# The delta rule's 128x128 inverse, by 32x32 diagonal squares in four corners of the array

## The chip, the cores and the metric

The kernel runs on one core of one Trainium2 chip. Its engines work side by side: TensorE (PE in the profile; PEld is its loading of weights), VectorE (DVE), ScalarE (ACT), GpSimd (POOL), and SyncE (SP), which starts most of the transfers. The metric is the time of one launch in device microseconds, the median of three runs.

## The reference

It is a trunk of two layers on a sequence of 256 tokens with 2048 channels, in float32. Each layer scales and shifts its normalised input by a modulation that is computed from `c`, mixes along the sequence, adds a gated residual, and follows with an MLP. Layer 0 mixes with eight heads of the gated delta rule and eight heads of chunk band attention, behind one combined input projection and ahead of one output projection; layer 1 mixes with a Mamba-2 scan (SSD). What the change touches is the triangular inverse in the delta rule:

```python
def gated_deltanet(q, k, v, z, b_raw, a_raw, conv_w, a_log, dt_bias, norm_w):
    ...
    lower = jnp.where(strict, jnp.einsum('bhnid,bhnjd->bhnij', kb, kc) * decay, 0.0)
    eye = jnp.eye(CHUNK, dtype=f32)
    tmat = lax.linalg.triangular_solve(eye + lower, jnp.broadcast_to(eye, lower.shape),
                                       left_side=True, lower=True, unit_diagonal=True)
    u = jnp.einsum('bhnij,bhnje->bhnie', tmat, vc * bc[..., None])
    w = jnp.einsum('bhnij,bhnjd->bhnid', tmat, kb * jnp.exp(gcum)[..., None])
    ...
def reference(x, c, mod_w, ...):
    c_act = jax.nn.silu(c)
    for layer in range(DEPTH):
        mod = jnp.einsum('bd,de->be', c_act, mod_w[layer]) + mod_b[layer]
        sh1, sc1, g1, sh2, sc2, g2 = [m[:, None, :] for m in jnp.split(mod, 6, axis=-1)]
        h = rms_norm(x, norm_mix_w[layer]) * (1.0 + sc1) + sh1
        ...
        x = x + g1 * mix
        h = rms_norm(x, norm_mlp_w[layer]) * (1.0 + sc2) + sh2
        x = x + g2 * sq_relu_mlp(h, mlp_w1[layer], mlp_w2[layer])
```

The kernel takes chunks of 128 tokens instead of the reference's 64, so that each of the eight heads has two 128x128 lower triangles to invert.

## The kernel before

**Projections.** Weights come in chunks of 1 MB (`raw`, four buffers, loaded by SP). Each chunk is split into a rounded half `wh` (ACT, a CAST, L332) and the rest `wl` (DVE, a subtraction, L336); the tokens' side is split in the same way (`u`). PE then multiplies (`mmx`, L322): 16 products of 512 columns with `wh`, which take both halves of `u` at once, and 16 of 256 columns with `wl`, which need only the rounded half of `u`. The name of the sum is `pw` or `pg`.

**The modulation** is not done on PE. A job (`mod_job`) loads 1 MB at a time into the same four `raw` buffers (`mraw`) and reduces each by one DVE instruction, L456. There are 192 of them over the kernel; `pump()` lets them go at a rate (`self.rate`, so many a quarter chunk) that is set stage by stage.

**What runs beside the projections.** A projection's chunk is issued in four quarters, with a `tick()` after each. A tick steps short tasks (`fast`), lets the background tasks take `bg_n` steps in turn (`bg_step`), and calls `pump()`. Background tasks are generators; each `yield` ends a step, and a step that yields `False` did nothing, so that the next task in turn is stepped. In the stage of the change `bg_n` is 1.5. A scheduler behind this then moves instructions within each engine's list by the readiness that it works out; the list that comes out is fixed, and each engine works through its own in order, with semaphores between them.

**The delta rule** is two background tasks, `gdn_group` 0 and 1, of four heads each; group 1 starts when group 0 is done. A group makes two tiles of 128 tokens (`gdn_tile`), each of which builds the strict lower triangle `gLt` for four heads (128x512) and inverts it: X starts as the identity minus the first subdiagonal of pairs, and level s (2, 4, 8, 16, 32, 64) joins blocks of s into blocks of 2s. Before, every level works on the full 128x128 of each head: a product of `gLt` and `gX` (L325 in `mm`), which DVE masks to the level's blocks (`gY`, L1131, after POOL has cleared the tile, L1130), a product with the transposed `gXt`, which DVE subtracts from X (L1137), then a transpose on PE (L329 in `tr`) and a copy by ACT into `gXt` (L1142). The last level goes into `gXt` straight away (L1146). The group goes on with `gvn`, `gS`, `gR`, `gqS` and `go`, whose transposes are the group's result; `gdn_z` puts the gate on it, and gives one of the four input units of the out projection. The flag `prep[0]` lets attention group 0 start.

**The out projection** takes its input units in the order 0, 2, 3, 1: a chunk holds two units, the first two chunks use units 0 and 2, and the third uses 3 (attention group 1) and 1 (delta rule group 1). `unit_of` steps a unit's tasks until they are done if its chunk comes first.

Of the kernel before, what the change touches and what calls it, by code (L numbers as in the profile page):

```python
# [12 lines left out]
I32 = mybir.dt.int32  # L13
AF = mybir.ActivationFunctionType
ALU = mybir.AluOpType
# [3 lines left out]
P = 128  # L19
# [93 lines left out]
class Trunk:  # L113
# [8 lines left out]
    def __init__(self, tc, ctx, ins, out):  # L122
# [14 lines left out]
        self.credit = self.fcredit = 0.0  # L137
        self.pending = self.early = self.etask = None
# [87 lines left out]

    def tick(self, quiet=False):
        self.fcredit = min(self.fcredit + self.fast_n, 3.0) if self.fast else 0.0
# [4 lines left out]
        n = len(self.bg)  # L233
# [167 lines left out]
    def masks(self):  # L401
        nc = self.nc
        g = nc.gpsimd
# [14 lines left out]

        self.M = {}
        for s in (2, 4, 8, 16, 32, 64):  # L420
            nb = P // (2 * s)
            m = self.const([P, nb, s], f"lev{s}")
            g.memset(m, 1.0)
            g.affine_select(out=m, in_=m, compare_op=ALU.is_ge, fill=0.0, base=-s, pattern=[[-2 * s, nb], [0, s]], channel_multiplier=1)
            g.affine_select(out=m, in_=m, compare_op=ALU.is_ge, fill=0.0, base=2 * s - 1, pattern=[[2 * s, nb], [0, s]], channel_multiplier=-1)
            self.M[s] = m

        self.M1T = self.const([P, 64, 2], "lev1T")
        g.memset(self.M1T, 0.0)
        v = self.M1T[:, :, 1:2]  # L430
        g.memset(v, 1.0)
        g.affine_select(out=v, in_=v, compare_op=ALU.is_equal, fill=0.0, base=0, pattern=[[-2, 64], [0, 1]], channel_multiplier=1)
        self.M1T = self.M1T.rearrange("p b c -> p (b c)")
# [613 lines left out]
    def gdn_tile(self, hg, t, kf, qf, vf, G):  # L1047
# [54 lines left out]

        xt = self.s2(tag="gXt")
        nc.vector.tensor_tensor(xt, lt, self.row(self.M1T), op=ALU.mult)
        nc.vector.tensor_tensor(xt, self.row(self.ident), xt, op=ALU.subtract)
# [8 lines left out]
        ps = self.pm()  # L1114
        for h in range(4):
            self.tr(ps[:, h], xt[:, h])
        x = self.s2(tag="gX")
        nc.scalar.copy(x, ps)
        G["X" + str(t)] = x
        yield  # L1120


        for s in (2, 4, 8, 16, 32, 64):
            nb = P // (2 * s)
            part = lambda a, n: a.rearrange("p h (b n c) -> p h b n c", n=2, c=s)[:, :, :, n]
            ps = self.pm()
            for h in range(4):
                self.mm(ps[:, h], lt[:, h], x[:, h])
            y = self.s2(tag="gY")
            nc.gpsimd.memset(y, 0.0)  # L1130
            nc.vector.tensor_tensor(part(y, 0), part(ps, 0), self.M[s].unsqueeze(1).to_broadcast([P, 4, nb, s]), op=ALU.mult)  # L1131
            yield
            ps = self.pm()
            if s < 64:
                for h in range(4):
                    self.mm(ps[:, h], xt[:, h], y[:, h])
                nc.vector.tensor_tensor(part(x, 0), part(x, 0), part(ps, 0), op=ALU.subtract)  # L1137
                yield
                ps = self.pm()
                for h in range(4):  # L1140
                    self.tr(ps[:, h], x[:, h])
                nc.scalar.copy(xt, ps)  # L1142
            else:
                for h in range(4):
                    self.mm(ps[:, h], y[:, h], xt[:, h])
                nc.vector.tensor_tensor(part(xt, 1), part(xt, 1), part(ps, 1), op=ALU.subtract)  # L1146
                yield
        G["Xt", t] = xt

    def gdn_group(self, hg, kc, qc, vc, gates):  # L1150
# [7 lines left out]
        while not all(t.done for t in tiles):  # L1158
            for t in tiles:
                if not t.done:  # L1160
                    t.step()
            if all("X" + str(n) in G for n in range(2)):
                self.prep[hg].done = True
            yield

# [659 lines left out]
```

## Time and profile before

| | us |
|---|---|
| median of three runs | 2698.53 (2694.78 to 2700.00) |
| the profiled execution, its own time | 2697.5 |
| its span | 2695.8 |
| PE busy in the span | 2638.6 (98%) |
| DVE busy in the span | 2154.2 (80%) |
| ACT busy in the span | 1348.0 (50%) |
| POOL busy in the span | 24.4 (1%) |
| mean granted clock of PE | 0.998 |

The profiler recorded one execution. Busy time is the time in which an engine works on at least one instruction; on PE many instructions are in flight at once, so a row's "mean ns of one" is a latency, and what one costs is the distance from one start to the next. Rows of groups read: line, engine, operation, output<-inputs by name, shape, count | busy us, mean ns of one | idle us of the engine just before them, and what ended most of it. Rows of waits read: engine, waiting tile and line <- engine, tile and line waited for: us in all, times, longest. Rows of the timeline read: start, duration, engine, instructions, count. Rows of stretches give for each engine the busy us and the instructions (x) in that stretch, then the granted clock and the share of the DMA engines.

### The profile page before, as it was taken

What the parts mean: (1) busy time and instruction counts of PE and PEld (TensorE: products, weight loads), DVE (VectorE), ACT (ScalarE), POOL (GpSimd) and SP (SyncE); (2) the same over time, 40 slices, a digit from 0 to 9 for tenths busy, and PEclk for the clock granted to TensorE, in tenths of its full rate; (3) what the DMA queues carried; (4) which work ended last, traced back from release to release, by engine and by line L of the source; (5) the groups of instructions that cost most, each with busy time, mean ns of one, the idle gap of its engine ahead of it and who ended that gap; (6) DMA issues with size and microseconds to landing.
All of it is one profiled execution on the core that took longest, in us unless ns stands there. A gap on an engine that the chain in (4) does not pass through costs nothing.

```text
span 2695.8 us, 40020 instructions
## 1 busy us (share of the span) xinstructions
PE 2638.6 (98%) x15834; PEld 2325.0 (86%) x15834; DVE 2154.2 (80%) x3106; ACT 1348.0 (50%) x1990; POOL 24.4 (1%) x98
## 2 busy tenths in 40 slices
PE   5999999999999999999999999999999999999999
PEld 4887989888888888888888888888888888888888
DVE  7998998997888888889889876897787855555554
ACT  3445455456345354454556544665555354454452
POOL 1000000000000000000000000000000000000000
PEclk9999999999999999999999999999999999999999
DMA  9986487868898898988555665554558855555553
GB/s 343 354 326 235 172 305 273 325 235 290 310 349 326 332 330 332 332 332 309 177 181 204 241 243 198 208 182 178 201 190 294 327 190 188 188 188 188 190 194 133
DMA packets 100459, 680.08 MB, mean 252 GB/s; under 512 B 11184, under 2 KB 14512, under 8 KB 19376
## 3 DMA queue, kind: packets, MB, share of 16 engines
q1 hardware_dynamic: 95376, 669.07, 68.0%
q10 hardware_dynamic: 4896, 8.46, 1.0%
q8 instruction: 124, 2.03, 0.3%
q14 instruction: 63, 0.52, 0.1%
HBM read 675.33 MB, written 2.16 MB: 251 GB/s over the span
## 4 chain that ended last, share of the span: by engine, by line
PE 91%; DVE 5%; DMA 1%; ACT 1%; issue 1%; SPq 0%; ACTq 0%; DVEq 0%
PE pw L322 71%; PE pg L322 13%; PE pm L325 3%; PE pm L322 2%; DVE mraw L456 2%; PE pm L329 1%; DVE wl L336 1%; DMA mraw<-in_mod_dram 1%; DVE u L1605 0%; ACT wh L332 0%; DVE hf L883 0%; DMA raw<-in_w_ab_dram 0%; DVE u L886 0%; DMA x<-in_x_dram 0%; DMA sd_rowd<-sd_rows 0%
## 5 line engine op out<-in xcount | busy, mean ns | idle before, releaser
L332 ACT CAST wh<-raw 128x1024 fp32r<-128x1024 f32 x870 | 906.0, 1051 | 999.4 <-PE pw L322 686.3
L336 DVE TENSOR_TENSOR wl<-raw,wh 128x1024 fp32r<-128x1024 f32 x870 | 1050.8, 1220 | 435.9 <-ACT wh L332 433.1
L322 PE MATMUL pw<-u,wh 128*128 128x512 f32 x5584 | 1320.0, 391 | 2.5 <-DVE u L886 1.3
L322 PEld LDWEIGHTS pw<-u,wh 128*128 128x128 f32 x5584 | 1031.9, 188 | 208.3 <-DVE x L948 1.5
L322 PEld LDWEIGHTS pw<-u,wl 128*128 128x128 f32 x5584 | 703.2, 192 | 21.8 <-issue 1.6
L322 PE MATMUL pw<-u,wl 128*128 128x256 f32 x5584 | 713.2, 284 | 0.7 <-DVE wl L336 0.7
L456 DVE SCALAR_TENSOR_TENSOR mraw<-mraw,crow 128x2048 f32<-128x2048 f32 x192 | 438.0, 2283 | 10.2 <-DMA mraw<-in_mod_dram 10.0
L322 PE MATMUL pg<-wh,u 128*128 128x512 f32 x864 | 278.8, 396 | 0.0
L322 PEld LDWEIGHTS pg<-wh,u 128*128 128x128 f32 x864 | 162.1, 188 | 32.7 <-issue 0.5
L948 DVE SCALAR_TENSOR_TENSOR x<-pw,mod,x 128x256 f32<-128x256 f32 x352 | 161.4, 478 | 33.0 <-PE pw L322 30.6
L322 PE MATMUL pg<-wl,u 128*128 128x512 f32 x432 | 170.0, 394 | 0.3 <-DVE wl L336 0.2
L322 PE MATMUL pg<-u,wh 128*128 128x256 f32 x672 | 124.5, 285 | 0.0
L322 PEld LDWEIGHTS pg<-u,wh 128*128 128x128 f32 x672 | 105.6, 192 | 0.3
L322 PEld LDWEIGHTS pg<-wl,u 128*128 128x128 f32 x432 | 81.3, 188 | 17.8 <-DVE wl L336 1.6
L322 PE MATMUL pg<-u,wl 128*128 128x256 f32 x336 | 95.4, 284 | 0.0
L322 PE MATMUL pm<-u,wh 128*128 128x256 f32 (+1 forms) x340 | 64.0, 292 | 19.2 <-ACT wh L332 19.2
L322 PEld LDWEIGHTS pm<-u,wh 128*128 128x128 f32 x340 | 54.2, 199 | 20.3 <-ACT wh L332 20.0
L322 PEld LDWEIGHTS pg<-u,wl 128*128 128x128 f32 x336 | 64.4, 192 | 0.0
L1007 DVE SCALAR_TENSOR_TENSOR u<-pad,cst,u 128x256 f32<-128x256 f32 x144 | 60.6, 479 | 4.7 <-ACT u L1001 4.7
L1511 ACT COPY rs<-pw 128x512 f32<-128x512 f32 x64 | 37.0, 578 | 34.5 <-PE pw L322 34.5
L885 ACT ACTIVATE u<-hf,mod 128x256 fp32r<-128x256 f32 x64 | 29.3, 502 | 48.4 <-DVE hf L883 48.4
L1512 DVE TENSOR_TENSOR rs<-pw,rs 128x512 f32<-128x512 f32 x64 | 43.8, 684 | 10.0 <-ACT rs L1511 10.0
(298 smaller groups left out, 1521.0 us busy)
## 6 DMA issues: line engine op xcount, KB each, us to landing
raw<-in_w_dram SPq DMA_DIRECT2D x256, 1024.0 KB, 5.1
mraw<-in_mod_dram SPq DMA_DIRECT2D x192, 1024.0 KB, 5.9
raw<-in_w_ab_dram SPq DMA_DIRECT2D x56, 1024.0 KB, 5.3
raw<-in_w_ssd_dram SPq DMA_DIRECT2D x48, 1024.0 KB, 4.9
raw<-in_w_sz_dram SPq DMA_DIRECT2D x32, 1024.0 KB, 4.9
raw<-in_wo_ssd_dram SPq DMA_DIRECT2D x32, 1024.0 KB, 4.9
raw<-in_wo_ab_dram SPq DMA_DIRECT2D x16, 1024.0 KB, 5.0
sE<-sd_rowd ACTq DMA_DIRECT2D x32, 256.0 KB, 4.2
```

The source lines that it names most:

```text
L322: return self.nc.tensor.matmul(o, a, b, start=start, stop=stop, skip_group_check=True)
L325: self.nc.tensor.matmul(o, lhsT, rhs, start=True, stop=True, skip_group_check=True)
L329: return self.nc.tensor.transpose(o, a, self.anti if flip else self.ident[:k, :k])
L332: a = self.nc.scalar.copy(hi, src)
L336: b = self.nc.vector.tensor_tensor(lo, src, hi.bitcast(F32), op=ALU.subtract)
L456: x = nc.vector.scalar_tensor_tensor(raw, raw, 1.0, self.crow, op0=ALU.mult, op1=ALU.mult, accum_out=t[:, f : f + 1])
L885: nc.scalar.activation(hi, h[:, f], AF.Identity, bias=shift[:, col])
L948: self.last = nc.vector.scalar_tensor_tensor(x[:, 2 * b + f], ps[:, f, n], g[:, 2 * cb + f : 2 * cb + f + 1], x[:, 2 * b + f], op0=ALU.mul ...
L1007: nc.vector.scalar_tensor_tensor(h, pad[:, f, 1 + q : 257 + q], w[:, q, j : j + 1], h, op0=ALU.mult, op1=ALU.add)
L1511: nc.scalar.copy(lo, ps[:, :, 1])
L1512: nc.vector.tensor_tensor(lo, ps[:, :, 0], lo, op=ALU.add)
```

## The change

`gdn_tile` ends when `gLt` and `gPt` are there. A new `gdn_inverse` then inverts both tiles of a group together, eight triangles at a time, and sets `G["Xt", t]` for the rest of the group, which is as before. It uses that X is block diagonal until level 16: only the four 32x32 squares on the diagonal are kept, one below the other, as a tile of 128x(8x32). Levels 2 to 16 multiply 32x32 squares, row group b of the array with column group b; DVE masks, subtracts and transposes (its own 32x32 transposes, in place of PE's). Level 32 joins pairs of squares, with four 32x32 corners written in place, and level 64 joins the two 64x64 halves. The masks are made once, and cut to their diagonal squares by copies on POOL. After each of its 13 steps the task yields `False` until three ticks have passed (`lag`), three quarters of a chunk; a task that is finished by force runs through up to 200 such yields a step without a tick. The flag `prep` is set after both tiles are done, ahead of the inverse.

```diff
--- before.py
+++ after.py
@@ -135,6 +135,7 @@
         self.fast, self.bg, self.open = [], [], []
         self.fast_n, self.bg_n = 0.5, 0.5
         self.credit = self.fcredit = 0.0
+        self.ticks = 0
         self.pending = self.early = self.etask = None
         self.pin = self.still = 0
         self.after_ins = self.gate = None
@@ -224,7 +225,16 @@
             t = self.fast.pop(0)
             t.finish()
 
+    def lag(self, n):
+
+        until = self.ticks + n
+        for _ in range(200):
+            if self.ticks >= until:
+                return
+            yield False
+
     def tick(self, quiet=False):
+        self.ticks += 1
         self.fcredit = min(self.fcredit + self.fast_n, 3.0) if self.fast else 0.0
         while self.fcredit >= 1:
             self.fcredit -= 1
@@ -416,21 +426,32 @@
+        def diagonal(name, full):
+
+            m = self.const([P, 32], name)
+            for b in range(4):
+                B = slice(32 * b, 32 * b + 32)
+                g.tensor_copy(m[B], full[B, B])
+            return m
+
+        self.I32 = diagonal("I32", self.ident)
...
+        for s in (2, 4, 8, 16):
+            full = self.s2([P, P], tag="lev")
...
+            self.M[s] = diagonal(f"lev{s}", full)
...
+        self.M1T = diagonal("lev1T", full)
@@ -1099,10 +1120,7 @@
         lt = self.s2(tag="gLt")
         for h in range(4):
             nc.vector.scalar_tensor_tensor(lt[:, h], ps[:, h], be[:, h : h + 1], E[:, h], op0=ALU.mult, op1=ALU.mult)
-
-        xt = self.s2(tag="gXt")
-        nc.vector.tensor_tensor(xt, lt, self.row(self.M1T), op=ALU.mult)
-        nc.vector.tensor_tensor(xt, self.row(self.ident), xt, op=ALU.subtract)
+        G["lt", t] = lt
         yield
         ps = self.pm()
         for h in range(4):
@@ -1111,41 +1129,89 @@
         nc.vector.tensor_tensor(p1, ps, E, op=ALU.mult)
         G["Pt", t] = p1
         yield
-        ps = self.pm()
-        for h in range(4):
-            self.tr(ps[:, h], xt[:, h])
-        x = self.s2(tag="gX")
-        nc.scalar.copy(x, ps)
-        G["X" + str(t)] = x
-        yield
-
-
-        for s in (2, 4, 8, 16, 32, 64):
-            nb = P // (2 * s)
-            part = lambda a, n: a.rearrange("p h (b n c) -> p h b n c", n=2, c=s)[:, :, :, n]
-            ps = self.pm()
-            for h in range(4):
-                self.mm(ps[:, h], lt[:, h], x[:, h])
-            y = self.s2(tag="gY")
-            nc.gpsimd.memset(y, 0.0)
-            nc.vector.tensor_tensor(part(y, 0), part(ps, 0), self.M[s].unsqueeze(1).to_broadcast([P, 4, nb, s]), op=ALU.mult)
-            yield
-            ps = self.pm()
-            if s < 64:
-                for h in range(4):
-                    self.mm(ps[:, h], xt[:, h], y[:, h])
-                nc.vector.tensor_tensor(part(x, 0), part(x, 0), part(ps, 0), op=ALU.subtract)
-                yield
-                ps = self.pm()
-                for h in range(4):
-                    self.tr(ps[:, h], x[:, h])
-                nc.scalar.copy(xt, ps)
+
+    def gdn_inverse(self, G):
+
+
+
+        nc = self.nc
+        lt = [G["lt", t] for t in range(2)]
+        heads = [(4 * t + h, t, h) for t in range(2) for h in range(4)]
+        B = [slice(32 * b, 32 * b + 32) for b in range(4)]
+        sub = [slice(4 * t, 4 * t + 4) for t in range(2)]
+        tile = lambda tag: self.s2([P, 8, 32], tag=tag)
+        flat = lambda a: a.rearrange("p n c -> p (n c)")
+        psum = lambda: self.pm([P, 512])[:, :256].rearrange("p (n c) -> p n c", c=32)
+        rep = lambda m, n: m.unsqueeze(1).to_broadcast([m.shape[0], n, 32])
+        xt, x = tile("gXt"), tile("gX")
+        for t in range(2):
+            for b in B:
+                nc.vector.tensor_tensor(xt[b, sub[t]], lt[t][b, :, b], rep(self.M1T[b], 4), op=ALU.mult)
+        nc.vector.tensor_tensor(xt, rep(self.I32, 8), xt, op=ALU.subtract)
+        nc.vector.transpose(flat(x), flat(xt))
+        XT = [self.s2(tag="gXT") for _ in range(2)]
+        x64 = self.s2([P, 8, 64], tag="gX6")
+        for z in XT:
+            nc.gpsimd.memset(z, 0.0)
+        nc.gpsimd.memset(x64[B[0], :, 32:], 0.0)
+        yield from self.lag(3)
+
+        for s in (2, 4, 8, 16):
+            ps = psum()
+            for n, t, h in heads:
+                for b in B:
+                    self.mm(ps[b, n], lt[t][b, h, b], x[b, n])
+            y = tile("gY")
+            nc.vector.tensor_tensor(y, ps, rep(self.M[s], 8), op=ALU.mult)
+            yield from self.lag(3)
+            ps = psum()
+            for n, t, h in heads:
+                for b in B:
+                    self.mm(ps[b, n], xt[b, n], y[b, n])
+            nc.vector.tensor_tensor(x, x, ps, op=ALU.subtract)
+            if s < 16:
+                nc.vector.transpose(flat(xt), flat(x))
             else:
-                for h in range(4):
-                    self.mm(ps[:, h], y[:, h], xt[:, h])
-                nc.vector.tensor_tensor(part(xt, 1), part(xt, 1), part(ps, 1), op=ALU.subtract)
-                yield
-        G["Xt", t] = xt
+                for t in range(2):
+                    for b in B:
+                        nc.vector.transpose(XT[t][b, :, b], x[b, sub[t]])
+            yield from self.lag(3)
+
+        ps = psum()
+        for n, t, h in heads:
+            for p in (0, 2):
+                self.mm(ps[B[p + 1], n], lt[t][B[p], h, B[p + 1]], x[B[p], n])
+        y = tile("gY")
+        for p in (0, 2):
+            nc.scalar.copy(y[B[p + 1]], ps[B[p + 1]])
+        nc.gpsimd.tensor_copy(x64[B[0], :, :32], x[B[0]])
+        nc.gpsimd.tensor_copy(x64[B[1], :, 32:], x[B[1]])
+        yield from self.lag(3)
+        ps = psum()
+        for n, t, h in heads:
+            self.mm(ps[B[1], n], XT[t][B[1], h, B[1]], y[B[1], n])
+            for p in (0, 2):
+                self.mm(ps[B[p], n], y[B[p + 1], n], XT[t][B[p + 1], h, B[p + 1]])
+        nc.vector.tensor_scalar(x64[B[1], :, :32], ps[B[1]], -1.0, None, op0=ALU.mult)
+        for t in range(2):
+            for p in (0, 2):
+                nc.scalar.activation(XT[t][B[p], :, B[p + 1]], ps[B[p], sub[t]], AF.Copy, scale=-1.0)
+        yield from self.lag(3)
+
+        lower, upper = slice(0, 64), slice(64, P)
+        ps = self.pm([P, 8, 64])
+        for n, t, h in heads:
+            self.mm(ps[upper, n], lt[t][lower, h, upper], x64[lower, n])
+        y = self.s2([P, 8, 64], tag="gY")
+        nc.scalar.copy(y[upper], ps[upper])
+        yield from self.lag(3)
+        ps = self.pm([P, 8, 64])
+        for n, t, h in heads:
+            self.mm(ps[lower, n], y[upper, n], XT[t][upper, h, upper])
+        for t in range(2):
+            nc.vector.tensor_scalar(XT[t][lower, :, upper], ps[lower, sub[t]], -1.0, None, op0=ALU.mult)
+            G["Xt", t] = XT[t]
+        yield from self.lag(3)
 
     def gdn_group(self, hg, kc, qc, vc, gates):
 
@@ -1159,9 +1225,9 @@
             for t in tiles:
                 if not t.done:
                     t.step()
-            if all("X" + str(n) in G for n in range(2)):
-                self.prep[hg].done = True
             yield
+        self.prep[hg].done = True
+        yield from self.gdn_inverse(G)
 
         ps = self.pm()
         for h in range(4):
```

The scheduler's lists then read as follows at three places. On PE, one level of group 0; `gX`, `gLt`, `gY`, `gXt` are the inverse's tiles, `pg` is a projection. Before:

```order
L329 MATMUL pm_2762<-ident,gX_2546 128x128 x4
L325 MATMUL pm_2768<-gX_2546,gLt_2495 128x128 x4
L329 MATMUL pm_2776<-ident,gX_2553 128x128 x4
L325 MATMUL pm_2782<-gX_2553,gLt_2508 128x128 x4
L322 MATMUL pg_2702<-hw_1725,raw_2557 128x256
L329 MATMUL pm_2790<-anti,as_2738 128x128
L322 MATMUL pg_2838<-wh_2686,u_286 128x512
...
L325 MATMUL pm_2806<-gY_2773,gXt_2500 128x128 x4
L325 MATMUL pm_2812<-gY_2787,gXt_2513 128x128 x4
```

After:

```order
L335 MATMUL pm_2909<-gX_2577,gLt_2521 32x32 x16
L335 MATMUL pm_2909<-gX_2577,gLt_2531 32x32 x16
L332 MATMUL pg_2870<-wh_2854,u_787 128x512
L332 MATMUL pg_2870<-wl_2855,u_787 128x512
L332 MATMUL pg_2870<-wh_2854,u_787 128x512
L332 MATMUL pg_2870<-wh_2858,u_788 128x512
...
L332 MATMUL pg_2870<-wl_2859,u_788 128x512
L335 MATMUL pm_2987<-gY_2942,gXt_2576 32x32 x32
L332 MATMUL pg_2870<-wh_2858,u_788 128x512 x2
```

The transposes are gone from PE, each product became 32 small ones, and the projection's products lie between the two steps of a level, since a step is three quarters of a chunk behind the last.

On PE, ahead of the out projection's third chunk, which writes the sum `pw_4819` before and `pw_5000` after; its inputs are the units 3 and 1 (`u_4931`, `u_4932`, `u_4857`, `u_4858` before; `u_5219`, `u_5220`, `u_5145`, `u_5146` after). Before:

```order
L322 MATMUL pw_4885<-u_4544,wl_4812 128x256 x4
L322 MATMUL pw_4885<-u_4545,wl_4812 128x256 x4
L322 MATMUL pw_4885<-u_4828,wl_4816 128x256 x4
L322 MATMUL pw_4885<-u_4829,wl_4816 128x256 x4
L322 MATMUL pw_4819<-u_4931,wl_4878 128x256 x4
L322 MATMUL pw_4819<-u_4932,wl_4878 128x256 x4
L322 MATMUL pw_4819<-u_4857,wl_4882 128x256 x4
L322 MATMUL pw_4819<-u_4858,wl_4882 128x256 x4
```

After:

```order
L335 MATMUL pm_5080<-gR_5068,gXT_4010 128x128 x3
L335 MATMUL pm_5088<-gvn_5054,gPt_3975 128x128 x3
L332 MATMUL pw_5173<-u_4617,wl_4993 128x256 x4
L335 MATMUL pm_5099<-gvn_5085,gPt_3982 128x128 x4
L332 MATMUL pw_5173<-u_5009,wl_4997 128x256 x4
L332 MATMUL pw_5173<-u_5010,wl_4997 128x256 x4
L339 MATMUL pm_5133<-ident,go_5093 128x128 x4
L339 MATMUL pm_5139<-ident,go_5104 128x128 x4
L332 MATMUL pw_5000<-u_5219,wl_5166 128x256 x4
L332 MATMUL pw_5000<-u_5220,wl_5166 128x256 x4
```

Before, the second chunk runs straight into the third. After, the end of group 1's chain (`gR` by `gXT`, `gvn` by `gPt`, the transposes of `go`) lies inside the second chunk and immediately ahead of the third.

On DVE, in the same place; `mraw` is the modulation job. Before:

```order
L456 SCALAR_TENSOR_TENSOR mraw_4919,mod_126<-mraw_4919,crow 128x2048
L1238 SCALAR_TENSOR_TENSOR cvt_4843<-cvt_4843,pg_4479 128x512
L1248 SCALAR_TENSOR_TENSOR u_2707<-cvt_4842,cst,u_2707 128x512
L1248 SCALAR_TENSOR_TENSOR u_2707<-cvt_4843,cst,u_2707 128x512
L336 TENSOR_TENSOR wl_4878<-raw_4875,wh_4877 128x1024
L336 TENSOR_TENSOR u_4857<-u_2707,u_4857 128x2x256
L336 TENSOR_TENSOR u_4858<-u_2707,u_4858 128x2x256
L336 TENSOR_TENSOR wl_4882<-raw_4875,wh_4881 128x1024
L336 TENSOR_TENSOR wl_4924<-raw_4921,wh_4923 128x1024
L336 TENSOR_TENSOR wl_4928<-raw_4921,wh_4927 128x1024
L336 TENSOR_TENSOR u_4931<-u_3463,u_4931 128x2x256
L336 TENSOR_TENSOR u_4932<-u_3463,u_4932 128x2x256
```

After:

```order
L287 SCALAR_TENSOR_TENSOR goy_5116<-got_5118,goy_5116 128x8
L1284 TENSOR_TENSOR goy_5116<-goy_5116,gor_5110 128x8
L1286 TENSOR_TENSOR go_5093<-go_5093,goy_5116 128x512
L1286 TENSOR_TENSOR go_5104<-go_5104,goy_5116 128x512
L477 SCALAR_TENSOR_TENSOR mraw_5412,mod_126<-mraw_5412,crow 128x2048
L1314 SCALAR_TENSOR_TENSOR u_2730<-cvt_5023,cst,u_2730 128x512
L1314 SCALAR_TENSOR_TENSOR u_2730<-cvt_5024,cst,u_2730 128x512
L346 TENSOR_TENSOR u_5145<-u_2730,u_5145 128x2x256
L346 TENSOR_TENSOR u_5146<-u_2730,u_5146 128x2x256
L346 TENSOR_TENSOR u_5219<-u_3375,u_5219 128x2x256
L346 TENSOR_TENSOR u_5220<-u_3375,u_5220 128x2x256
```

Before, the delta rule's rows lie far above. After, its last rows (`goy`, `go`) and a modulation instruction stand just ahead of the splits of `u` that the third chunk needs; the splits `wl` of that chunk stand far above them. By these rows DVE has issued 69 modulation instructions before and 73 after.

More of the change, by code (lines that the diff above doesn't have):

```diff
@@ L417, in masks @@
         g.affine_select(out=self.anti, in_=self.anti, compare_op=ALU.is_equal, fill=0.0, base=1 - P, pattern=[[1, P]], channel_multiplier=1)
+        def diagonal(name, full):
[5 more added lines that the diff above has]
+        self.I32 = diagonal("I32", self.ident)
         self.M = {}
-        for s in (2, 4, 8, 16, 32, 64):
+        for s in (2, 4, 8, 16):
+            full = self.s2([P, P], tag="lev")
+            v = full.rearrange("p (b n c) -> p b n c", n=2, c=s)[:, :, 0]
             nb = P // (2 * s)
[L422 to L430, printed above, removed]
+            g.memset(full, 0.0)
+            g.memset(v, 1.0)
+            g.affine_select(out=v, in_=v, compare_op=ALU.is_ge, fill=0.0, base=-s, pattern=[[-2 * s, nb], [0, s]], channel_multiplier=1)
+            g.affine_select(out=v, in_=v, compare_op=ALU.is_ge, fill=0.0, base=2 * s - 1, pattern=[[2 * s, nb], [0, s]], channel_multiplier=-1)
+            self.M[s] = diagonal(f"lev{s}", full)
+        full = self.s2([P, P], tag="lev")
+        v = full.rearrange("p (b c) -> p b c", c=2)[:, :, 1:2]
+        g.memset(full, 0.0)
         g.memset(v, 1.0)
         g.affine_select(out=v, in_=v, compare_op=ALU.is_equal, fill=0.0, base=0, pattern=[[-2, 64], [0, 1]], channel_multiplier=1)
-        self.M1T = self.M1T.rearrange("p b c -> p (b c)")
+        self.M1T = diagonal("lev1T", full)
     def mod_start(self, layer):
@@ L1113, in gdn_tile @@
         yield
-        ps = self.pm()
-        for h in range(4):
-            self.tr(ps[:, h], xt[:, h])
-        x = self.s2(tag="gX")
-        nc.scalar.copy(x, ps)
-        G["X" + str(t)] = x
-        yield
-        for s in (2, 4, 8, 16, 32, 64):
-            nb = P // (2 * s)
-            part = lambda a, n: a.rearrange("p h (b n c) -> p h b n c", n=2, c=s)[:, :, :, n]
-            ps = self.pm()
-            for h in range(4):
-                self.mm(ps[:, h], lt[:, h], x[:, h])
-            y = self.s2(tag="gY")
-            nc.gpsimd.memset(y, 0.0)
-            nc.vector.tensor_tensor(part(y, 0), part(ps, 0), self.M[s].unsqueeze(1).to_broadcast([P, 4, nb, s]), op=ALU.mult)
-            yield
-            ps = self.pm()
-            if s < 64:
-                for h in range(4):
-                    self.mm(ps[:, h], xt[:, h], y[:, h])
-                nc.vector.tensor_tensor(part(x, 0), part(x, 0), part(ps, 0), op=ALU.subtract)
-                yield
-                ps = self.pm()
-                for h in range(4):
-                    self.tr(ps[:, h], x[:, h])
-                nc.scalar.copy(xt, ps)
-            else:
-                for h in range(4):
-                    self.mm(ps[:, h], y[:, h], xt[:, h])
-                nc.vector.tensor_tensor(part(xt, 1), part(xt, 1), part(ps, 1), op=ALU.subtract)
-                yield
```

## The prediction

> **What bounds the kernel now.** I read the page's shares first, then busy time by stretch, then what DVE waits for, and last the instructions on either side of one moment.
>
> ```profile
> PE 2638.6 (98%) x15834; PEld 2325.0 (86%) x15834; DVE 2154.2 (80%) x3106; ACT 1348.0 (50%) x1990; POOL 24.4 (1%) x98
> ```
>
> By this line PE is the bound: work taken from it would come off the time one for one. The share is a mean, though, so the stage that the change touches has to be looked at by itself. The two groups of the delta rule lie between about 262 and 497 us.
>
> ```profile
> core 0: us, PE busy (x) PEld busy (x) DVE busy (x) ACT busy (x) POOL busy (x), PEclk, DMA share, GB/s
> 262.00:497.00 235.00, 232.20 (x1612) 211.71 (x1611) 220.34 (x451) 121.13 (x282) 12.75 (x31) 1.00 0.70 253
> 497.00:570.00 73.00, 73.00 (x420) 64.55 (x419) 71.95 (x102) 34.78 (x46) 0.00 (x0) 1.00 0.92 340
> 570.00:600.00 30.00, 27.39 (x163) 24.28 (x161) 25.93 (x61) 16.79 (x30) 0.00 (x0) 0.94 0.47 171
> ```
>
> In the stage PE is busy 232.2 of 235 us, and DVE 220.3: two engines are nearly full, and DVE has 14.7 us of slack. This is what it waits for there:
>
> ```profile
> DVE wl L336 <- ACT wh L332: 5.3, 8, 1.5
> DVE gR L1183 <- PE pm L325: 2.0, 1, 2.0
> DVE as L1313 <- issue: 1.7, 1, 1.7
> DVE ass L1270 <- ACT pg L1267: 1.6, 1, 1.6
> DVE gvn L1170 <- PE pm L325: 1.0, 1, 1.0
> DVE mraw L456 <- DMA mraw<-in_mod_dram: 0.6, 1, 0.6
> DVE gY L1131 <- PE pm L325: 0.6, 3, 0.2
> DVE goss L1214 <- ACT pm L1208: 0.4, 1, 0.4
> ```
>
> The squares' own chain (gY) waits 0.6 us in all: other work lies in its gaps. The largest wait, 5.3 us for the rounded half of a weight chunk, is a wait for PE at one remove, since ACT may write wh only when PE has done with the buffer.
>
> The stage ends where the third chunk of the out projection starts:
>
> ```profile
> 489.62 3.82 PE L322 MATMUL pw<-u,wh 128*128 128x512 f32 x16
> 492.85 3.48 DVE L336 TENSOR_TENSOR wl<-raw,wh 128x1024 fp32r<-128x1024 f32 x3
> 493.27 4.12 PE L322 MATMUL pw<-u,wl 128*128 128x256 f32 x33
> 496.26 1.28 DVE L336 TENSOR_TENSOR u<-u,u 128x512 fp32r<-128x512 f32 x2
> 497.22 3.82 PE L322 MATMUL pw<-u,wh 128*128 128x512 f32 x16
> ```
>
> The last two rows are the point. The wide products at 497.22 need the first of the two DVE instructions at 496.26, which ends at about 496.9. So DVE hands over 0.3 us before PE asks: the engines reach the end of the stage together. A chunk costs PE 16 x 0.228 (489.62 to 493.27) + 16 x 0.120 (33 in 3.95) = 5.55 us, and from here to 570 PE is busy 73.00 of 73.00. Each engine's instructions after about 600 us stand in the same order in both kernels, so the change is worth the shift of this one point.
>
> **What PE sheds.**
>
> ```profile
> 275.02 1.86 PEld L325 LDWEIGHTS pm<-gX,gLt 128*128 128x128 f32 x16
> 276.81 0.53 PEld L325 LDWEIGHTS pm<-u,u 128*128 128x128 f32 x4
> ...
> L325 PE MATMUL pm<-gX,gLt 128*128 128x128 f32 x192 | 25.2, 275 | 0.0
> L325 PE MATMUL pm<-gY,gXt 128*128 128x128 f32 x160 | 20.0, 275 | 0.0
> L325 PE MATMUL pm<-gXt,gY 128*128 128x128 f32 x32 | 4.1, 275 | 0.0
> L329 PE MATMUL pm<-ident,gX 128*128 128x128 f32 x80 | 12.3, 273 | 0.0
> L329 PE MATMUL pm<-ident,gXt 128*128 128x128 f32 x16 | 2.4, 274 | 0.0
> ```
>
> The 275 ns of one are latency; sixteen start within 1.79 us (275.02 to 276.81), 0.112 each. 192 + 160 + 32 + 96 = 480 instructions go, 53.7 us of PE.
>
> In their place come 592 products of 32x32 and 32 of 64x64; a float32 product is two instructions here (192 for 96 products), so 1184 and 64. Before has none of these shapes. Nearest are the 64-column products of the second layer:
>
> ```profile
> 1397.79 1.29 PE L322 MATMUL pw<-u,wh 128*128 128x512 f32 x5
> 1399.01 1.15 PE L325 MATMUL pm<-sx,sE 128*64 128x64 f32 x32
> 1400.10 2.11 PE L322 MATMUL pw<-u,wh 128*128 128x512 f32 x8
> ```
>
> 32 start in 1.09 us, 0.034 each, with entering and leaving the narrow shape inside it. I take half for half the columns, 0.016: 1184 x 0.016 = 18.9; the 64x64 ones at 0.034 give 2.2. Entering and leaving: five wide ones ahead of that group should take 5 x 0.228 = 1.14 and take 1.22, and eight behind take 1.94 (to the next start at 1402.04) instead of 1.82, so at least 0.2 us is lost a visit. There are 24 visits and about four split ones; at 0.2 to 0.35 that is 6 to 10, taken as 9. Together 30 us, so PE sheds about 23. Ends: at 0.008 a square, 33; at 0.034, 2; at 0.068 (twice the row: the small shape gains nothing and no square runs beside another), a loss of 40.
>
> [...]
>
> **What DVE sheds and gets.**
>
> ```profile
> L1131 DVE TENSOR_TENSOR gY<-pm,lev 128x256 f32<-128x256 f32 x24 | 9.8, 417 | 0.6 <-PE pm L325 0.6
> L1137 DVE TENSOR_TENSOR gX<-gX,pm 128x256 f32<-128x256 f32 x20 | 8.1, 413 | 0.2
> L1146 DVE TENSOR_TENSOR gXt<-gXt,pm 128x256 f32<-128x256 f32 x4 | 1.6, 414 | 0.0
> L1104 DVE TENSOR_TENSOR gXt<-gLt,lev1T 128x512 f32<-128x512 f32 x4 | 2.7, 684 | 0.0
> L1105 DVE TENSOR_TENSOR gXt<-ident,gXt 128x512 f32<-128x512 f32 x4 | 2.7, 681 | 0.0
> L1101 DVE SCALAR_TENSOR_TENSOR gLt<-pm,gbe,gE 128x128 f32<-128x128 f32 x16 | 5.0, 342 | 0.0
> L456 DVE SCALAR_TENSOR_TENSOR mraw<-mraw,crow 128x2048 f32<-128x2048 f32 x192 | 438.0, 2283 | 10.2 <-DMA mraw<-in_mod_dram 10.0
> ```
>
> The first five rows go: 9.8 + 8.1 + 1.6 + 2.7 + 2.7 = 24.9. Added are 64 instructions: 32 of 256 elements a lane at 0.414 = 13.2, and 32 of 128 at 0.342 (L1101, a dearer form) = 10.9; 24.1, or a little less. I take a net -2. Of the 64, 24 are transposes, an operation that no row shows; priced like the others they are 8 x 0.414 + 16 x 0.342 = 8.8. Ends: half (-4.4) and double (+8.8). [...]
>
> The order brings a larger term. The pacing pushes group 1's last levels and all that follows them into the first two chunks of the out projection, forced there since the third needs its result. More of the modulation job has been let through by then: ahead of the third chunk's splits DVE has 73 of the L456 instructions, against 69 before. That is 4 x 2.283 = +9.1 us of DVE work ahead of the point that ends the stage, and four more 1 MB loads ahead of it on SP's queue; the DMA share of 0.70 has room for 4 MB more in 235 us (17 GB/s on 253).
>
> **The other queues.**
>
> ```profile
> L1142 ACT COPY gXt<-pm 128x512 f32<-128x512 f32 x20 | 11.7, 583 | 15.9 <-PE pm L329 15.8
> L1118 ACT COPY gX<-pm 128x512 f32<-128x512 f32 x4 | 2.3, 582 | 5.7 <-PE pm L329 5.7
> mraw<-in_mod_dram SPq DMA_DIRECT2D x192, 1024.0 KB, 5.9
> ```
>
> ACT loses these copies (14.0 us) and gets seven a group back, six of them at most half as wide, under 6 us; at 121 of 235 us it paces nothing. POOL loses 24 memsets and gets ten small operations, and is busy 12.75 of 235 us. The masks' extra copies stand at the start of the kernel, far ahead of what uses them. The last row is the load that each of the four L456 instructions brings along. No instruction waits for `lag` itself: it only changes the order.
>
> **The sum.** DVE work to the point: 220.3 + 9.1 - 2.0 = 227.4 us. Slack: the 5.3 and the 1.7 go, as PE now is some 23 us lighter than DVE's pace needs; the rest that has a name is 2.0 + 1.6 + 1.0 + 0.6 + 0.6 + 0.4 = 6.2, and it stays, because the forced tail has the same steps (gvn, gR, goss), with large splits and modulation between most of them. I add 0.6 for the rounding on ACT that DVE's last four instructions now wait for, since the tail ends immediately ahead of them. 262 + 227.4 + 6.2 + 0.6 = 496.2, against 496.9: -0.7 us. PE's side is 262 + 232.2 - 23 + 2.8 = 474: PE would wait for DVE. The profiled execution took 2697.5 us, 1.0 below the median of the runs, so the forecast is 2697: PE's saving turns into PE waiting.
>
> **The rivals.**
> - PE's saving counts. For it speaks PE's 98%; against it, that DVE cannot finish its list before 262 + 227.4 = 489.4 with no slack at all, so at most 7.5 us can come, 2690; with transposes at their lower end 4.4 more, 2685. Only if DVE's instructions themselves ran faster, say for want of POOL's 12.75 us beside them, would the full 23 show: 2675.
> - A transpose costs half of what its neighbours do: -0.7 - 4.4 = -5.1, 2692. Nothing in the profile speaks for or against it. [...]
> - The tail is serial. Levels 16, 32 and 64 and eight more steps hand over between PE, ACT and DVE with nothing but two chunks beside them. If DVE's slack stays at 14.7 in spite of a faster PE, the point moves to 262 + 227.4 + 14.7 + 0.6 = 504.7, +7.8: 2705; with transposes at double, 2714. It turns slower once the slack passes 13 us. At 570 to 600, where the next layer part starts, PE idles 2.6 of 30 us and the granted clock is 0.94: a longer PE idle could cost clock as well.
> - The squares don't run beside each other, and the change doesn't do what it says. At 0.034 each PE ends at 262 + 232.2 - 2 + 2.8 = 495, beside DVE, and the forecast stands; at 0.068 it has 262 + 232.2 + 40 + 2.8 = 537: +40, 2737. It is slower than DVE from about 0.036 on. [...]
>
> **How the numbers follow.** About 0.2%, 5.4 us, is what a measurement here can tell: faster is below 2693.1, slower above 2703.9. DVE's pace with slack between 3 and 12: 0.58, itself 2693 to 2702. The transposes cheap or the slack nearly gone, 2685 to 2693: 0.20. The full PE gain: 0.05. The serial tail: 0.12. Squares at over 0.04 us: 0.05. The first spills over both bounds, by 0.08 to the fast side and 0.05 to the slow one. Faster 0.33, same 0.45, slower 0.22. The range is 2685 to 2707; the full PE gain, the far part of the serial tail and the slow squares stay outside.
>
> **What would show it.** If I am right: PE's busy share between 262 and 497 falls from 0.988 to about 0.9, with PE idle put down to DVE (wl and u); DVE's share rises to 0.96 or more; the third chunk's wide products start at 496 to 497; each level takes PE about 1.0 us for its 64 square instructions. Wrong: the stretch from 497 on begins 5 us earlier or later, a transpose far from 0.41 us, or 64 squares in 3 us.

## The result, and the profile after

The changed kernel takes 2717.8 us (median of six runs, 2716.0 to 2719.0), 1.0074 times the kernel before, 95% interval 1.0064 to 1.0084: about 20 us slower, where 2697 and at most 2707 were forecast. The profiled execution has a span of 2716.9 us.

The shares of the page say nothing of it. PE has shed 10 us over the whole kernel and DVE is as busy as before:

```profile
PE 2628.6 (97%) x16602; PEld 2301.7 (85%) x16602; DVE 2155.6 (79%) x3114; ACT 1342.3 (49%) x1980; POOL 30.2 (1%) x106
```

The stage ended before where the third chunk's wide products start, at 497.22 us; now they start at 517.14, 19.9 us later. Busy time by stretch, cut at 513, just before PE takes up the third chunk; the last row ends with DVE's last split of `u` for that chunk, at 514.9:

```profile
core 0: us, PE busy (x) PEld busy (x) DVE busy (x) ACT busy (x) POOL busy (x), PEclk, DMA share, GB/s
262.00:513.00 251.00, 218.04 (x2360) 185.23 (x2358) 227.19 (x465) 111.66 (x268) 7.12 (x15) 0.91 0.69 257
262.00:480.00 218.00, 196.63 (x2184) 166.48 (x2182) 199.60 (x411) 99.79 (x235) 7.12 (x15) 0.93 0.70 264
480.00:513.00 33.00, 21.42 (x177) 18.75 (x177) 27.59 (x55) 11.87 (x33) 0.00 (x0) 0.78 0.58 213
513.00:570.00 57.00, 56.44 (x313) 50.15 (x314) 49.17 (x68) 26.03 (x37) 0.00 (x0) 0.95 0.69 257
262.00:514.92 252.92, 219.40 (x2366) 186.59 (x2365) 229.11 (x468) 112.97 (x272) 7.12 (x15) 0.91 0.69 258
```

To its last split of `u` DVE is busy 229.1 us, and 227.4 were forecast; but it idles 252.9 - 229.1 = 23.8 us, and 6.8 were forecast. Of these, 18.4 us (218.0 - 199.6) lie ahead of 480 us and 5.4 between 480 and 513. PE idles too, 11.6 of 33 us in the last stretch, and its granted clock there is 0.78. In both kernels the work can be followed by DVE's splits wl, which come in the same number and order. Two stretches between the same splits, the 59th to the 105th (which opens the second chunk of the out projection), and the 105th to the 113th (four chunks on), before:

```profile
213.50:483.70 270.20, 266.42 (x1773) 234.67 (x1771) 248.21 (x545) 137.56 (x368) 13.48 (x34) 1.00 0.67 246
483.70:507.10 23.40, 23.40 (x137) 20.74 (x137) 22.47 (x28) 13.68 (x21) 0.00 (x0) 1.00 0.92 333
```

and after:

```profile
212.80:470.80 258.00, 235.93 (x2233) 195.21 (x2232) 231.69 (x506) 119.32 (x326) 6.95 (x18) 0.94 0.69 259
470.80:528.10 57.30, 45.16 (x446) 38.75 (x445) 44.66 (x86) 24.42 (x56) 1.72 (x2) 0.82 0.50 178
```

At the 105th split the changed kernel is 12.9 us ahead, with 16.5 us of DVE's work put off; eight splits later it is 21.0 behind. Counted on DVE's list, which adds up the loss but doesn't explain it, of these 21.0 DVE's work is 5.7 (276.4 against 270.7, most of it modulation moved ahead), its idle time 4.3 in the first stretch and 11.7 in the second, less 0.7 at the start. The largest waits of PE and of DVE between 480 and 517 us:

```profile
PE pm L339 <- DVE go L1286: 6.1, 1, 6.1
PE pw L332 <- ACT u L342: 4.2, 1, 4.2
DVE wl L346 <- ACT wh L342: 2.8, 1, 2.8
DVE mraw L477 <- DMA mraw<-in_mod_dram: 0.8, 1, 0.8
```

and the same place in the timeline, where the chain of PE, ACT and DVE can be read line by line:

```profile
500.07 1.19 PE L332 MATMUL pw<-u,wl 128*128 128x256 f32 x8
501.54 2.29 DVE L477 SCALAR_TENSOR_TENSOR mraw<-mraw,crow 128x2048 f32<-128x2048 f32 x1
502.90 0.19 ACT L1274 ACTIVATION_READ_ACCUMULATOR pm<-go 128x1 f32 x1
503.75 0.16 DVE L1280 TENSOR_TENSOR goss<-goss,gor 128x8 f32<-128x8 f32 x1
...
506.56 1.29 DVE L1286 TENSOR_TENSOR go<-go,goy 128x512 f32<-128x512 f32 x2
507.40 1.94 PE L339 MATMUL pm<-ident,go 128*128 128x128 f32 x8 [6.14 <-DVE go L1286]
508.71 2.29 DVE L477 SCALAR_TENSOR_TENSOR mraw<-mraw,crow 128x2048 f32<-128x2048 f32 x1 [0.85 <-DMA mraw<-in_mod_dram]
509.38 0.59 ACT L1294 COPY u<-pm 128x512 f32<-128x512 f32 x1 [0.27 <-PE pm L339]
510.92 1.41 DVE L1314 SCALAR_TENSOR_TENSOR u<-cvt,cst,u 128x512 f32<-128x512 f32 x2
511.70 2.33 ACT L342 CAST u<-u 128x512 fp32r<-128x512 f32 x4 [1.74 <-DVE u L1314]
513.56 3.78 PE L332 MATMUL pw<-u,wl 128*128 128x256 f32 x16 [4.22 <-ACT u L342]
517.14 4.68 PE L332 MATMUL pw<-u,wh 128*128 128x512 f32 x16
```

PE runs dry at 501.3, waits for the normalisation of go, transposes it, and waits again for the gated and rounded u. The first wait, 6.1 us, is a row of small steps: ACT's sums of squares, the last of which ends at 503.09, small DVE instructions of 0.2 us each from 503.75 to 506.56, and the first of the two that write `go`. DVE also has a modulation instruction of 2.3 us each time ahead of what PE waits for (501.54, 508.71), but most of each is hidden: by these rows the first holds the chain up by about 0.7 us (503.09 to 503.75), the second by about 0.95 (from the end of ACT's copy, 509.97, to 510.92).

### The profile page after: what moved, and what is told of

The parts are those of the page before. It is cut to its first block, busy times and chain, and to the rows that moved or that the text cites. A ratio compares the mean times of both kernels' runs of the same rounds, so it can differ in the third digit from the quotient of the medians.

```text
span 2716.9 us, 41519 instructions
## 1 busy us (share of the span) xinstructions
PE 2628.6 (97%) x16602; PEld 2301.7 (85%) x16602; DVE 2155.6 (79%) x3114; ACT 1342.3 (49%) x1980; POOL 30.2 (1%) x106
## 4 chain that ended last, share of the span: by engine, by line
PE 87%; DVE 8%; ACT 1%; issue 1%; DMA 1%; DVEq 0%; ACTq 0%
PE pw L332 70%; PE pg L332 12%; DVE mraw L477 3%; PE pm L332 2%; PE pm L335 2%; DVE wl L346 2%; PE pm L339 1%; DMA mraw<-in_mod_dram 1%; ACT wh L342 0%; DVE u L1671 0%; DVE hf L904 0%; ACT pm L1086 0%; DVE u L907 0%; ACT u L906 0%; DMA sE<-sd_rowd 0%
```

## The experiments

Each run is given as its ratio to the kernel before, with the 95% interval. The second and third columns of the tables are the two stretches above, each as its length in us and DVE's idle time in it: two numbers from one row of the busy times of that run's trace.

### Lag and products, crossed

The lag's length in the changed kernel, none (a plain yield), one, two or three ticks; and the kernel before with the lag of three:

```diff
 # changed kernel, 13 places
-        yield from self.lag(3)
+        yield                     # nolag;   self.lag(1) in lag1, self.lag(2) in lag2
 # b_lag3: kernel before, in the loop over the levels
-            yield
+            yield from self.lag(3)
 # and in gdn_group, so that a lag of both tiles is passed on
-            yield
+            yield any(ok)
```

> The small squares with a plain yield behind each of the 13 steps instead of a lag of three ticks. Theory (the tail: the lag puts group 1's last steps immediately ahead of the third chunk of the out projection, and PE, DVE and ACT wait for one another there): the transposes of go now stand some 190 rows of PE ahead of that chunk, so PE waits under 2 us between 480 and 515 (14 in the changed kernel), and the time is 2685 to 2697. Rival clock (PE with less to do is granted a lower clock, and pays for it through the stage, wherever the tail lies): granted clock about 0.91 in the stage as in the changed kernel, time 2710 or more. Rival price (DVE's and ACT's small instructions of the inverse cost more than they save): 2705 or more.

> The small squares with a lag of one tick instead of three. Theory (the tail): the transposes of go stand some 210 rows of PE ahead of the third chunk, as good as without a lag, 2685 to 2697. Rival clock: 2710 or more. Rival price: 2705 or more.

> The small squares with a lag of two ticks. The transposes of go stand 19 rows of PE ahead of the third chunk, in its first chunk instead of at the end of its second. Theory (the tail): in between, part of the wait remains, 2695 to 2708. Rivals clock and price: like the changed kernel, 2712 or more.

> The kernel before with its 128x128 products and transposes, each of its level steps behind a lag of three ticks. The transposes of go stand immediately ahead of the third chunk, as in the changed kernel. Theory (the tail): the pacing alone makes it slow, and since PE keeps its 54 us of inverse, slower than the changed kernel or equal: 2712 to 2735. Rival clock: PE has its full work, so its clock stays near 1.00 and the time near before, 2695 to 2703. Rival price: no small instruction is there, 2695 to 2703.

| run | 59th to 105th split: us, DVE idle | 105th to 113th: us, idle | median us | ratio |
|---|---|---|---|---|
| before | 270.2, 22.0 | 23.4, 0.9 | 2697.5 | |
| changed (lag 3) | 258.0, 26.3 | 57.3, 12.6 | 2717.8 | 1.0074 (1.0064 to 1.0084) |
| lag2 | 271.2, 32.5 | 50.7, 13.0 | 2719.9 | 1.0082 (1.0067 to 1.0097) |
| lag1 | 284.0, 34.4 | 23.4, 0.9 | 2712.0 | 1.0052 (1.0037 to 1.0067) |
| nolag | 277.7, 29.2 | 24.7, 2.2 | 2707.1 | 1.0033 (1.0022 to 1.0045) |
| b_lag3 | 270.6, 25.8 | 41.8, 8.4 | 2714.3 | 1.0059 (1.0043 to 1.0076) |

The second stretch does what the tail theory says: 8 to 13 us of idle DVE with a lag of two or three, also with the old products (b_lag3), and 0.9 to 2.2 without. b_lag3, which has no small square, rules out both rivals for its own loss: they had it at 2695 to 2703. But nolag and lag1 are not back at 2685 to 2697, as the tail theory also said: DVE idles 7 to 12 us more than before in their first stretch. The rival of the price had 2705 or more for both, and its number came true; the runs with other values of bg_n, further down, ask whether its cause did. lag2, expected in between, is as slow as the changed kernel.

### PE's load and PE's clock

In b_half the products of the levels read rounded inputs, so that each is one PE instruction instead of two (192 instead of 384); otherwise every row of PE and DVE stays in its place. The two fills give PE idle products behind 20 groups of squares, without lag and with it.

```diff
 # b_half: gLt, gX, gXt, gY as float32r tiles
-        lt = self.s2(tag="gLt")
+        lt = self.s2(dt=F32R, tag="gLt")
...
 # fills, behind each group of 32x32 squares
+            for _ in range(4):
+                self.mm(self.spare, self.ident, self.ident)
```

> The kernel before, with the 384 product instructions of the inverse's levels cut to half by rounded inputs (one pass instead of two; the inverse is then less exact, which this run doesn't look at). Every row of PE and of DVE stands in the same order as before, so PE sheds 192 x 0.112 = 21.5 us in the stage, as much as the change was to shed, and nothing else changes: no lag, no squares, no tail. Theory (DVE and the chains pace the stage, PE's saving turns into waiting): 2691 to 2699. Rival clock (a lighter PE is granted a lower clock and pays for it): slower than before, 2703 to 2710, with a granted clock of 0.95 or less between 262 and 497 us. Rival PE (PE's work is the bound, and what the new order does to it is the loss): 2676 to 2685.

> The small squares without lag, with four idle 128x128 products (8 instructions, 0.9 us) behind each of the 20 groups of 32x32 squares, into a spare part of their PSUM tile: 18 us of PE work that nobody reads, about what the change took away. The order of the rest is nearly as without them. Rival clock (PE's waits lower its granted clock, and the products that follow pay): the clock in the stage rises from 0.91 to 0.97 or more, and the time falls below that of the kernel without lag (2707) to 2697 to 2704. Theory (order: the list puts work of ACT and DVE ahead of the casts and splits that PE needs, and clock is only its sign): the same 2707 or up to 10 us more.

> The changed kernel with the same idle products behind its 20 groups of 32x32 squares. Theory (the tail is serial and forced ahead of the third chunk): no faster than the changed kernel, 2714 to 2728, and PE waits for go and for u ahead of the third chunk as in it (6.1 and 4.2 us). Rival clock: 2708 or less.

| run | 59th to 105th: us, idle | 105th to 113th: us, idle | median us | ratio |
|---|---|---|---|---|
| b_half | 267.4, 20.1 | 23.4, 0.9 | 2695.9 | 0.9994 (0.9985 to 1.0004) |
| nolag_fill | 278.7, 30.0 | 25.1, 2.7 | 2708.5 | 1.0043 (1.0028 to 1.0058) |
| after_fill | 269.0, 26.5 | 46.8, 12.5 | 2717.3 | 1.0072 (1.0055 to 1.0089) |

The row of b_half's first stretch against that of before: PE busy 251.4 us instead of 266.4, DVE 247.3 instead of 248.2.

```profile
214.10:481.50 267.40, 251.42 (x1581) 214.62 (x1579) 247.34 (x546) 137.92 (x368) 13.37 (x34) 0.99 0.68 248
```

The 192 instructions are 21.5 us at 0.112 each, and 15.0 of busy time. The stretch is 2.8 us shorter, the whole is not: taken from an engine that is 98% busy, they are worth nothing that can be measured. The fill speaks against the clock: without lag it rose between 262 and 500 us from 0.91 to 0.97, as that rival asked, and the time did not fall. It is no clean test, since the fill is also some 18 us of work; but PE still idles 18 of the 238 us.

```profile
262.00:500.00 238.00, 209.72 (x2338) 180.22 (x2338) 214.71 (x451) 110.49 (x267) 4.10 (x15) 0.91 0.66 247
262.00:500.00 238.00, 219.63 (x2493) 190.49 (x2491) 213.31 (x450) 108.91 (x263) 4.18 (x15) 0.97 0.66 243
```

(The first row is the kernel without lag, the second the same with fill.)

### DVE's load, and another order of the same work

```diff
 # b_half_mod: b_half, and in mod_job for layer 0's second to fourth modulations
-  x = nc.vector.scalar_tensor_tensor(raw, raw, 1.0, self.crow, ...)
+  x = nc.vector.scalar_tensor_tensor(raw[:, :1024], raw[:, :1024], 1.0, self.crow[:, :1024], ...)
 # b_bg12, b_bg20 (kernel before), nolag_bg20 (squares without lag)
-        self.bg_n = 1.5
+        self.bg_n = 1.2           # or 2.0
```

> The kernel before with one-pass products in the levels (PE 21.5 us lighter), and with the 48 modulation instructions of layer 0 that run between about 262 and 575 us cut to half their width, so that half of those sums is left out: 1.1 us of DVE less for each, some 36 us ahead of the third chunk of the out projection. Theory (DVE paces the stage): now PE's saving counts, and the time falls by 12 to 22 us, to 2675 to 2685. Rival (hand-overs between the engines pace it, neither engine's load): 2690 or more.

> The kernel before with bg_n 1.2 instead of 1.5 in the stage: the background tasks are stepped more slowly, the work is the same, only the lists differ. It asks what an arbitrary other order costs. Theory (the order by itself is worth some us either way): a time more than 3 us off 2697, either side. Rival (the squares cost what the lists lose: DVE's and ACT's hand-overs of the inverse): within 3 us of 2697.

> The kernel before with bg_n 2.0: the same question with faster steps. Theory (order): more than 3 us off 2697. Rival (squares): within 3 us of 2697.

> The small squares without lag, with bg_n 2.0. Theory (order): no closer than 3 us to the 2707 of bg_n 1.5, either side. Rival (squares): 2704 to 2710.

b_half_mod leaves out half of each of those modulation sums. The time stays, 2697.9 us, ratio 0.9999 (0.9990 to 1.0008): DVE was busy 214.2 us in the first stretch instead of 248.2, and idled 58.0 instead of 22.0. The expected 12 to 22 us didn't come. Shorter instructions also change the order that the scheduler chooses (some hundreds of rows of PE's list), so this run can't say what DVE's load would be worth in the old order: what the new order costs could hide a gain. The others are in the table below.

### Is it the squares or the order

The only edit is again bg_n, for both kinds of products.

> The kernel before with bg_n 1.45 instead of 1.5: the same instructions, some hundred rows of DVE's list in another place. Theory (the list: the new order of instructions, whatever is in it, costs DVE idle time; the list of before is an exceptionally good one): 2702 to 2715, with DVE's work to the third chunk within 3 us of before and the difference in its idle time. Rival (squares: a list is as good as another, and the squares' hand-overs are the loss): 2694 to 2701.

> The same with bg_n 1.55. Theory (the list): 2700 to 2712. Rival (squares): 2694 to 2701.

> The small squares without lag with bg_n 1.45. Theory (the list): a time scattered like that of the 128x128 products under other values of bg_n, 2700 to 2715. Rival (squares): some 8 us over the 128x128 products with the same bg_n.

> The small squares without lag, bg_n 1.4: one more list. Theory (the list): anywhere from 2692 to 2715, with DVE's idle time to the third chunk explaining the difference to before within 3 us. Rival (squares): within 3 us of 2694.

> The small squares without lag and with bg_n 1.45 once more, in five rounds: the one list so far that is no slower than before. If it is a better list, and not a lucky run: 2691 to 2697 and an interval that ends below 1.000.

| bg_n | 128x128 products (before): first stretch us, DVE idle | median us, ratio | squares without lag: first stretch us, DVE idle | median us, ratio |
|---|---|---|---|---|
| 1.2 | 284.2, 32.1 | 2713.4, 1.0056 (1.0041 to 1.0071) | | |
| 1.4 | | | 261.9, 20.5 | 2696.3, 0.9997 (0.9988 to 1.0006) |
| 1.45 | 273.7, 23.7 | 2702.8, 1.0018 (1.0008 to 1.0027) | 260.7, 18.0 | 2694.3, 0.9987 (0.9977 to 0.9996); again, five rounds: 2695.2, 0.9992 (0.9983 to 1.0001) |
| 1.5 | 270.2, 22.0 | 2697.5 | 277.7, 29.2 | 2707.1, 1.0033 (1.0022 to 1.0045) |
| 1.55 | 278.1, 28.3 | 2709.0, 1.0039 (1.0024 to 1.0054) | | |
| 2.0 | 275.3, 24.7 | 2705.4, 1.0028 (1.0016 to 1.0039) | 286.7, 37.7 | 2713.4, 1.0059 (1.0044 to 1.0074) |

With the same instructions, the four other orders of the kernel before are 5 to 16 us slower than it, and DVE's work differs by at most 4 us in the first stretch. The squares without lag scatter over the same range, from 2694 to 2713, and at 1.45 they are 8 us faster than the old products. The squares at 1.45 are below both guesses, and the run at 1.4 fits both. So the 9.6 us of nolag don't belong to the squares as such: they are what this order costs against that one. The fastest order found is level with the kernel before, by its five rounds.

What the order does can be seen in PE's waits for the levels' own tiles (262 to 520 us without lag at 1.5):

```profile
PE pm L335 <- DVE gY L1165: 5.1, 5, 1.5
PE pm L335 <- DVE gX L1171: 5.0, 3, 1.8
```

and at 1.45 (262 to 540 us), where L1171 is not among them:

```profile
PE pm L335 <- DVE gY L1165: 0.7, 2, 0.5
```

At 1.5 most of these waits (9.2 us) fall between 405 and 422 us: there the squares' chain stands bare, with no projection in its gaps. Late weights alone don't tell the two orders apart: from 395 to 416 us ACT waits 17.5 us for chunks at 1.5, and 18.7 at 1.45.

### Where the lag may stand

```diff
 # g0lag: group 0 with lag 3, group 1 with a plain yield;  after_bg145: changed kernel, bg_n 1.45
-        yield from self.lag(3)
+        yield from self.lag(3 if hg == 0 else 0)     # lag(0): one plain yield
```

> The changed kernel with the lag of three ticks in group 0 alone; group 1's steps have a plain yield. The transposes of go stand 19 rows of PE ahead of the third chunk, in the first chunk of the out projection and early in the second. Theory (the forced tail of group 1 costs about 10 us of the 20): 2705 to 2712. Rival (lag costs wherever it is; the tail is no worse than another place): 2714 to 2722.

> The changed kernel, lag of three ticks, with bg_n 1.45. Theory (with a lag the tail is forced ahead of the third chunk in every list; the rest is the luck of the list): DVE idles 8 us or more while it splits the last four half chunks up to the third chunk, as in the other lists with a lag, and the time is 2708 to 2728. Rival (only luck of the list, lag or not): as good as without lag at this bg_n, 2692 to 2700.

| run | 59th to 105th: us, idle | 105th to 113th: us, idle | median us | ratio |
|---|---|---|---|---|
| g0lag | 273.4, 32.1 | 47.9, 13.6 | 2722.7 | 1.0091 (1.0076 to 1.0106) |
| after_bg145 | 263.0, 27.9 | 47.5, 5.9 | 2712.1 | 1.0057 (1.0043 to 1.0071) |

Both are against a detail of the theory. In g0lag the second stretch didn't shrink: attention steps now stand in it as well, and PE waits there 5.5 us for their DVE tiles (as) beside 3.1 for go. With the lag at bg_n 1.45 the idle time in the second stretch is 5.9 us, not 8, though that stretch is 14 us longer than without lag. Every order with a lag of two or more, six of six with after_fill, has a second stretch of 42 to 57 us; every order with less has 23 to 35. With bg_n and the products the same, the lag of three costs 10.7 us (the changed kernel against nolag), 16.8 (b_lag3 against before) and 16.8 (after_bg145 against nolag in its five rounds). Each of these pairs changes the order too, so how much of it is the tail alone is not shown.

## Why the prediction was wrong

**What held.** PE's saving was worth nothing (b_half). DVE's work was 229.1 us, against 227.4, with the 73 modulation instructions in it. The inverse's DVE rows:

```profile
L1177 DVE STREAM_TRANSPOSE gXT<-gX 32x128 f32<-32x128 f32 x16 | 4.8, 302 | 0.2
L1173 DVE STREAM_TRANSPOSE gXt<-gX 128x256 f32<-128x256 f32 x6 | 2.6, 440 | 0.0
L1149 DVE TENSOR_TENSOR gXt<-gLt,lev1T 32x128 f32<-32x128 f32 x16 | 4.5, 282 | 0.2
```

A transpose of 256 costs 0.440 and one of 128 costs 0.302 (0.414 and 0.342 were taken), so both ends of that term fall. The 128 elements more cost 138 ns; if the first 128 went at that rate, an estimate from these two rows, some 164 ns of each instruction would not depend on its length.

**The squares were too dear in the sum.** 0.016 us each was taken. The loads of one group, and what follows:

```profile
318.66 0.64 PEld L335 LDWEIGHTS pm<-gX,gLt 32*32 32x32 f32 x64 [0.35 <-issue]
319.34 0.19 PEld L332 LDWEIGHTS pg<-wh,u 128*128 128x128 f32 x1
```

and the products around them:

```profile
318.34 0.39 PE L332 MATMUL pg<-wh,u 128*128 128x512 f32 x1
318.66 0.75 PE L335 MATMUL pm<-gX,gLt 32*32 32x32 f32 x64
319.34 0.50 PE L332 MATMUL pg<-wh,u 128*128 128x512 f32 x1
319.68 0.39 PE L332 MATMUL pg<-wl,u 128*128 128x512 f32 x1
```

64 start in 0.68 us, 0.011 each, as in most groups; the first two groups took 1.0 us. The loads idle 0.35 us ahead of them, but the price on PE is less: the wide products on either side take 0.32 and 0.34 us to the next start instead of 0.228, so entering and leaving cost about 0.2 together, the lower end of what was taken. At the pace of a wide product (0.228 us for 512 columns) 32 columns would take 0.014, an estimate; these squares, which all write one tile (`pm`), start closer together than that, so they seem to overlap at least in part. No run isolates it. It helped nothing, since PE's load doesn't count here.

**The step that failed** is the slack: "the rest that has a name is 2.0 + 1.6 + 1.0 + 0.6 + 0.6 + 0.4 = 6.2, and it stays, because the forced tail has the same steps". It was 23.8 with the rounding's 0.6 inside it: 17.0 us more than the 6.8 of the sum. DVE's work adds 1.7 us (229.1 for 227.4). The rest is PE's: from DVE's last split, at 514.9, to the wide products at 517.14 it is 2.2 us, since the narrow products are still running, where the forecast had 0.3. So 17.0 + 1.7 + 1.9 turn the forecast of -0.7 into the measured 19.9. The largest waits inside the 23.8:

```profile
DVE wl L346 <- ACT wh L342: 7.6, 6, 2.8
DVE gvn L1236 <- PE pm L335: 4.0, 1, 4.0
DVE gss L1091 <- ACT pm L1086: 3.6, 1, 3.6
```

Three things were wrong in it.
- "The 5.3 and the 1.7 go": the wait for the rounded half of a chunk did not go with a lighter PE. It is 7.6 us, the largest of all.
- The tail is serial: the rival of that name, with a chance of 0.12 and priced at 2705, took place in part, at 2718. From 480 us on DVE idles 5.4 us, where before it idled 0.9, and PE waits 10.4 us for go and u. The runs with a lag show 5.9 to 13.6 us of idle DVE in the second stretch, against 0.9. That modulation stands between the chain's steps doesn't cover the chain but adds about 1.6 us to it.
- The rest of the slack, 18.4 us ahead of 480 where before had 13.8, was read as a property of the work, waits that stay or go one by one. It is a property of the order: gvn's 4.0 and gss's 3.6 us fall at 358 and 393 us, long before the tail. The kernel before has 22.0 us in the first stretch; other orders of the same instructions have 23.7 to 32.1. Any edit that makes the scheduler order this stage anew draws again: of the nine other orders here with a lag of one tick or none, seven were slower than the kernel before and two level with it (the fills and b_half_mod, which change the work, are not counted). The forecast had no term for that.

**Not shown in cause:** "DVE's pace" forecast the time of b_half, but with 34 us less of DVE work as well (b_half_mod) the time stayed, in another order. In the order of before, PE's load doesn't set the time; for DVE's load that is open. How the lists of PE, DVE and ACT meet is worth 5 to 16 us by itself. What makes the order of the kernel before, or of the squares at 1.45, a good one is open; no run isolates it.

## What to carry to other kernels

Where two engines are both above 90% busy (here PE for 232.2 and DVE for 220.3 of 235 us) and work through fixed lists, take neither's saved time as gain until a run with the order unchanged shows that it is one; rounding the inputs of the products, which halved the PE instructions of those products and moved no row, was such a run. Price a change that makes a scheduler order anew with the scatter of the order itself: run the old kernel with its step rate a few per cent off, here 5 to 16 us. And a lag that spreads steps out puts work off; count what is left when the first consumer forces it, and assume that chain runs in sequence (here PE waited 10.4 us for go and u), with whatever the engine's list holds in between.

## What the runs showed of the hardware

The stage's mean granted clock of 0.91 hides how far it falls for some microseconds. In the changed kernel, PE, clock, DMA share and GB/s alone:

```profile
500.00:510.00 10.00, 3.20 (x19) 0.77 0.65 238
510.00:520.00 10.00, 6.44 (x25) 0.55 0.29 106
520.00:530.00 10.00, 10.00 (x53) 1.00 0.29 105
```

After waits of 6.1 and 4.2 us the 16 narrow products at 513.56 took 3.58 us, 0.224 each, instead of 0.120: nearly half speed, and 1.7 us on the path. What a higher clock would be worth in the tail is open: with the fill and the lag PE still waits there, 6.0 us for go and 3.3 for u. Without a tail the fill raised the clock of the stage to 0.97, and the time was no shorter (2708.5 us with it, 2707.1 without).
